# Decays of a Mamba-2 branch from running sums: one DMA per group repeats them on all partitions, instead of matmuls per pair of heads

## The chip, the core and the metric

One NeuronCore of a Trainium2 chip runs the kernel alone. The metric is device time in microseconds, from runs of the whole kernel. Five engines work side by side, each through its own queue in order: PE (TensorE, matmuls), DVE (VectorE) and ACT (ScalarE) for elementwise work, POOL (GpSimd) for elementwise work in SBUF, and SP, which here only issues DMAs.

## What is computed

The reference is one layer of a decoder block on 256 tokens of 2048 features: a sliding-window attention and a Mamba-2 (SSD) branch side by side, then a ConvFFN and a gated embedding. The change lies in the SSD branch alone, which has 64 heads of 64 features in 8 groups of 8 heads, a state of 128, and two chunks of 128 tokens:

```python
a = jnp.moveaxis(dt * A, 2, -1)
a_cum = jnp.cumsum(a, axis=-1)
xdt = x * dt[..., None]
seg = jnp.exp(jnp.where(causal, a_cum[..., :, None] - a_cum[..., None, :], -jnp.inf))
cb = jnp.einsum('bclgn,bcsgn->bcgls', Cm, Bm)
y_diag = jnp.einsum('bcgjls,bcsgjp->bclgjp', cb[:, :, :, None] * seg, xdt)
decay_to_end = jnp.exp(a_cum[..., -1:] - a_cum)
chunk_states = jnp.einsum('bclgn,bcgjl,bclgjp->bcgjpn', Bm, decay_to_end, xdt)
y_off = jnp.einsum('bclgn,bcgjpn,bcgjl->bclgjp', Cm, states_in, jnp.exp(a_cum))
```

`seg` is, for each head, a 128 x 128 matrix of decays between two tokens of a chunk: the exponential of a difference of running sums of `a`. `exp(a_cum)` is the decay from the start of a chunk to each of its tokens.

## The kernel before

All large products are float32 and are made of two matmuls in a rounded format: a weight chunk of 512 KB is loaded (`raw`, five buffers), ACT rounds it (`wh`, three buffers, L77), DVE takes the rest (`wl`, three buffers, L78), and PE multiplies `wh` with both halves of the activations (512 columns, L84) and `wl` with one half (256 columns, L83 or L86). `panel` makes two tiles of 128 features from four such chunks of eight pairs of matmuls; every part of the layer runs through it.

The SSD branch is a loop over 8 groups (L292). Each takes five panels: two for x, one for B and C together, two for the gate z. A panel of x, B or C is evicted by `conv`, with ACT's copy `lo` (L282) first; one of z by `summed` (L112). `step_sizes` (L226) runs once beside the first panels and gives `dt`, `dta` (dt times A, by token) and its rounded halves `dhl`.

For chunk c of a group the kernel then makes E, the decays of all 8 heads (tokens s on the partitions, tokens l along the columns). For each half of four heads and each half of `dhl`, POOL multiplies the mask `tri` with `dhl`, both broadcast, into `rm` (L345, 128 x 512, two buffers), and PE multiplies a strictly lower triangular matrix with it (L347). Their sum in PSUM is the difference of the running sums, and ACT's exponential puts it into E (L348). DVE multiplies E with the masked product of C and B (`cbm`, L349), PE multiplies with `xdt` (L353, eight fp32 matmuls), and DVE adds the skip term (L357).

For the path from chunk 0 into chunk 1, PE makes `po` from the state (L365), and with eight fp32 matmuls (L370) the running sums of chunk 1 for each pair of heads, repeated over 64 partitions each; ACT takes their exponential `ec` (L373), and DVE multiplies and adds (L374, L375). Then follow the gate (L386), the group norm (ACT's square L387, POOL's sums of it L388 and L389, two matmuls L392, POOL's power L396, two matmuls L399, DVE L400) and the split into `YS`.

The order of the instructions on each engine is not the program's: a scheduler with a model of time lays it out (`schedule_with_timeline_sim=True`), so that the small matmuls of the SSD stand among the pairs of the panels. A DMA that ACT issues stands in ACT's queue, and waits there for what it needs.

Of the kernel before, what the change touches and what calls it, by code (L numbers as in the profile page):

```python
# [17 lines left out]
P = 128  # L18
T = 256
# [18 lines left out]
RLEN = 384  # L38
# panels of queries and of gate_a: attention on one pair of heads runs beside the panels that follow it
ATT_ORDER = ([("q", 0), ("q", 1), ("q", 2)] + [x for n in range(5) for x in (("g", n), ("q", n + 3))]  # L40
# [4 lines left out]
def hybrid_block(ctx: ExitStack, tc: tile.TileContext, a: dict, out: bass.AP):  # L45
# [46 lines left out]
    def panel(src, base, nk, xs, before=None, between=None, joined=False):  # L92
        """Two feature tiles of w.T @ x: halves [w*x_hi + w_lo*x_hi | w_hi*x_lo], or joined in one half."""
        ps = [acc(), acc()]
        for j in range(nk // KC):
            if before:
                wh, wl = load_chunk(src[base + j], parts=2, before=lambda i, j=j: before(KC * j + 2 * i))
            else:
                wh, wl = load_chunk(src[base + j])
            for ct in range(2):  # L100
                cs = slice(ct * P, (ct + 1) * P)
                for k in range(KC):
                    (products_joined if joined else products)(
                        ps[ct], wh[:, k, cs], wl[:, k, cs], xs[:, j * KC + k, :],
                        j * KC + k == 0, j * KC + k == nk - 1)
            if between:
                between()
        return ps
# [8 lines left out]
    def split(dst, src):  # L117
        """dst[:, 0:T] + dst[:, T:2T] == src, each part with 12 significant bits."""
        S.activation(dst[:, 0:T], src, AF.Copy)
        V.tensor_tensor(dst[:, T:2 * T], src, dst[:, 0:T].bitcast(F32), ALU.subtract)  # L120
# [7 lines left out]

# [1 line left out]
    g_mix = load_const("g_mix", [P, ND])  # L130
# [22 lines left out]
    def stat_to_rstd(sq_blocks, name):  # L153
        """Rows' mean squares -> [P, 2] rstd by token and [P, T] broadcast over partitions."""
        st = misc()
# [41 lines left out]

# [1 line left out]
    y_pool = tc.alloc_tile_pool(name="yp", bufs=1)  # L199
    YS = y_pool.tile([P, 4 * GROUPS, 2 * T], F32R, name="YS")  # L200
    with tc.tile_pool(name="ssm", bufs=2) as sp:
# [3 lines left out]
        nc.sync.dma_start(sl32, a["slow"])  # L205
        slr = sp.tile([P, P], F32R, name="slr", bufs=1)
        V.tensor_copy(slr, sl32)
        cw = sp.tile([P, 48, 4], F32, name="cw", bufs=1)
# [9 lines left out]

        # dt = softplus(raw + bias), by token
        H = SSM_HEADS  # L220
        dt = sp.tile([P, 2, H], F32, name="dt", bufs=1)
        dta = sp.tile([P, 2, H], F32, name="dta", bufs=1)
        dtd = sp.tile([P, H], F32, name="dtd", bufs=1)
        dhl = sp.tile([P, 2, 2, H], F32R, name="dhl", bufs=1)

        def step_sizes():  # L226
# [25 lines left out]
            for b in range(2):  # L252
                V.scalar_tensor_tensor(xr[:, b, :], psd[:, b * H:(b + 1) * H], r_tok[:, b:b + 1], dtb,
                                       ALU.mult, ALU.add)
            # softplus(x) = max(x, 0) + log1p(e), e = exp(-|x|); log1p(e) = 2 atanh(e / (2 + e))
            e = scr[:, 6 * P:7 * P].rearrange("p (b h) -> p b h", b=2)
# [15 lines left out]
            V.scalar_tensor_tensor(dta, dt, -1.0, bc(ea.unsqueeze(1), [P, 2, H]), ALU.mult, ALU.mult)  # L272
            S.activation(dhl[:, 0], dta, AF.Copy)
            V.tensor_tensor(dhl[:, 1], dta, dhl[:, 0].bitcast(F32), ALU.subtract)
            pst = misc()
# [16 lines left out]
        for g in range(GROUPS):  # L292
            hs = slice(8 * g, 8 * g + 8)
            xc = sp.tile([P, 4, T], F32, name="xc")
            for pn in range(2):
                if g + pn == 0:
                    ps2 = first
                else:
                    ps2 = panel(W, base, ND, XS)
                    base += CH  # L300
                if g + pn == 0:
                    step_sizes()
                for i in range(2):
                    j = 2 * pn + i
                    conv(ps2[i], 4 * g + j, xc[:, j, :])
# [7 lines left out]

            # C.B for s in chunk 0 (both chunks of l), then chunk 1
            pcb = misc()
# [6 lines left out]

            # x by token, times dt
            xdt = sp.tile([P, 2, 512], F32, name="xdt", bufs=1)
# [13 lines left out]
            for c in range(2):  # L338
                E = sp.tile([P, 8, P], F32, name="E", bufs=1)
                for hf in range(2):  # L340
                    h4 = slice(8 * g + 4 * hf, 8 * g + 4 * hf + 4)
                    pe = misc()
                    for w in range(2):
                        rm = sp.tile([P, 4, P], F32R, name="rm", bufs=2)
                        G.tensor_tensor(rm, bc(tri.unsqueeze(1), [P, 4, P]),  # L345
                                        bc(dhl[:, w, c, h4].bitcast(F32).unsqueeze(2), [P, 4, P]), ALU.mult)
                        TE.matmul(pe, lhsT=slr, rhs=rm, start=(w == 0), stop=(w == 1))  # L347
                    S.activation(E[:, 4 * hf:4 * hf + 4, :], pe.rearrange("p (h l) -> p h l", h=4), AF.Exp)  # L348
                V.tensor_tensor(E, E, bc(cbm[:, 2 * c, :].unsqueeze(1), [P, 8, P]), ALU.mult)  # L349
# [9 lines left out]

            # from chunk 0 into chunk 1  # L360
            po = misc()
            pc = misc()
            for j in range(4):
                js = slice(j * P, (j + 1) * P)
                TE.matmul(po[:, js], lhsT=xde[:, js], rhs=cbm[:, 1, :], start=True, stop=True)  # L365
            for j in range(4):
                js = slice(j * P, (j + 1) * P)
                for r in range(2):
                    hd = 8 * g + 2 * j + r
                    TE.matmul(pc[r * HD:(r + 1) * HD, js], lhsT=bc(dta[:, 1, hd:hd + 1], [P, HD]),  # L370
                              rhs=tri, start=True, stop=True)
            ec = sp.tile([P, 512], F32, name="ec", bufs=1)
            S.activation(ec, pc, AF.Exp)  # L373
            V.tensor_tensor(ec, po, ec, ALU.mult)  # L374
            V.tensor_tensor(yg[:, :, P:T], yg[:, :, P:T], ec.rearrange("p (j l) -> p j l", j=4), ALU.add)  # L375

            # gate and group norm
            zg = sp.tile([P, 4, T], F32, name="zg", bufs=2)
# [25 lines left out]

    # gate_s, then the SSD branch's output projection
    t1_pool = tc.alloc_tile_pool(name="t1", bufs=1, side="right")
# [14 lines left out]

# [1 line left out]
    m_pool = tc.alloc_tile_pool(name="mp", bufs=1, side="right")  # L423
# [3 lines left out]
    with tc.tile_pool(name="att", bufs=2) as ap:  # L427
        # bias[q, h, j] for key j of [own block | previous block], each block's keys from last to first;
        # masked outside the window
        tab = ap.tile([N_BUCKETS + 1, N_HEADS], F32, name="tab", bufs=1)  # L430
# [27 lines left out]
        def head_rstd(t, scale, nm):  # L458
            """[P tok, blk, 2 heads]: scale * r / sqrt(r^2 ms + eps) for a tile of two heads."""
            sq = ap.tile([P, T], F32, name="hsq")  # L460
# [14 lines left out]
        def by_token():  # L475
            """A panel's 256 features by token."""
            nonlocal base
# [13 lines left out]

        # keys: normalised, both gains folded in, reversed in each block (block 1 first),
        # copied to both halves of the partitions
        flip = ap.tile([P, P], F32, name="flip", bufs=1)
# [27 lines left out]

        # values by token, reversed in each block
        vt = ap.tile([P, 2, 256], F32, name="vt", bufs=1)
# [8 lines left out]
        def attend(i, qc):  # L533
            """One pair of heads, in steps that are laid between the chunks of later panels."""
            g = i // 4
            bias = pair_bias(i)
            rq = head_rstd(qc, HD ** -0.5, "rq")
            Ls = ap.tile([P, 2, 384], F32, name="Ls", bufs=3)
            # head h: its high part on its own half of the partitions, the low part on the other half
            Q = ap.tile([P, 2, T], F32R, name="Q")  # L540
# [74 lines left out]

    # attention's output projection and the mix
    ms_pool2 = tc.alloc_tile_pool(name="mp2", bufs=1, side="right")
# [13 lines left out]

# [1 line left out]
    x_pool = ctx.enter_context(tc.tile_pool(name="xp", bufs=1))  # L633
# [56 lines left out]

# [1 line left out]
    with tc.tile_pool(name="ple", bufs=2) as pp:  # L692
# [36 lines left out]
def _bucket_onehot():  # L729
    """[33, 384]: column v stands for distance v - 127; the last row marks what lies outside the window."""  # L730
    d = np.arange(MAX_DISTANCE)
# [15 lines left out]
def _panels(w, cols):  # L747
    """w's columns, 256 a panel, as [panels * k-chunks, 128, KC * 256]."""
    k = w.shape[0]
# [15 lines left out]
def _layout(i):  # L765
# [10 lines left out]
    w_in = i["w_in"][0]  # L776
    two = lambda v: np.concatenate([v, v]).reshape(P, 1)  # noqa: E731
    m = {
# [52 lines left out]
```

## Time and profile before

| | before |
|---|---|
| time, median of 3 runs (lowest to highest) | 2137.7 us (2135.12 to 2138.09) |
| span of the profiled execution, first to last instruction | 2133.4 us |
| busy, share of the span: PE, DVE, ACT, POOL | 99%, 71%, 55%, 9% |
| mean granted TensorE clock, share of full speed | 0.996 |
| DMA traffic | 377.04 MB, mean 177 GB/s |

The times are of runs without a profile; of the profiled execution the span is known, and it stands 4.3 us below the median. In the profile's views, the busy time of PE is the sum of its matmul records, which overlap. An fp32 matmul makes two records. The chain of work that ended last follows the program back from its end, at each step to what released it. The idle time of an engine is given with the instruction that ended it. The loop over the SSD groups lies between about 35 and 615 us of the span.

### The profile page before, as it was taken

How to read it: one execution, taken by the hardware profiler on the slowest of the kernel's cores; microseconds unless marked ns; L12 is line 12 of the kernel's file. 1: busy time of each engine (PE TensorE's matmuls, PEld its weight loads, DVE VectorE, ACT ScalarE, POOL GpSimd, SP SyncE). 2: the span in 40 equal slices, each digit the busy share in tenths (PEclk: the TensorE clock that was granted, in tenths of full speed). 3: DMA queues.
4: the chain of work that ended last, by engine and by line, in shares of the span. 5: the costliest groups of instructions: out<-in, count | busy, mean ns of one | idle time of the engine just before them, and what ended most of it. 6: DMA issues, size and time to landing. Idle time of an engine off the chain costs nothing.

```text
span 2133.4 us, 32471 instructions
## 1 busy us (share of the span) xinstructions
PE 2114.2 (99%) x12412; PEld 1833.4 (86%) x12412; DVE 1508.8 (71%) x2528; ACT 1174.8 (55%) x1783; POOL 181.7 (9%) x154
## 2 busy tenths in 40 slices
PE   7999999999999999999999999999999999999999
PEld 5888888888888889888888888888888888888888
DVE  7788888888654455766677677777777776555576
ACT  5665666656554444656565556555555555444454
POOL 3221222211100000000000020000000000000000
PEclk9999999999999999999999999999999999999999
DMA  5444444444455556444435655555555555555564
GB/s 196 168 168 164 164 159 158 166 167 165 154 191 187 186 185 201 153 161 139 160 119 178 227 187 184 191 188 186 186 189 188 186 187 187 188 187 188 178 206 145
DMA packets 112072, 377.04 MB, mean 177 GB/s; under 512 B 13931, under 2 KB 20908, under 8 KB 111788
## 3 DMA queue, kind: packets, MB, share of 16 engines
q1 hardware_dynamic: 104060, 366.00, 49.3%
q10 hardware_dynamic: 7856, 8.97, 1.3%
q8 instruction: 97, 1.59, 0.3%
q14 instruction: 59, 0.48, 0.1%
HBM read 372.78 MB, written 2.15 MB: 176 GB/s over the span
## 4 chain that ended last, share of the span: by engine, by line
PE 99%; DVE 1%; ACT 0%; issue 0%; DMA 0%; POOL 0%; DVEq 0%; ACTq 0%
PE acc L84 59%; PE acc L86 29%; PE acc L83 2%; PE ms L550 1%; PE ms L347 1%; PE ms L353 1%; PE ms L549 1%; PE ms L582 1%; PE acc L90 1%; PE ms L365 0%; PE ms L370 0%; PE ms L589 0%; PE acc L486 0%; PE ms L84 0%; PE acc L487 0%; PE acc L488 0%
## 5 line engine op out<-in xcount | busy, mean ns | idle before, releaser
L78 DVE TENSOR_TENSOR wl<-raw,wh 128x1024 fp32r<-128x1024 f32 (+1 forms) x700 | 863.7, 1234 | 507.3 <-ACT wh L77 495.4
L77 ACT ACTIVATE wh<-raw 128x1024 fp32r<-128x1024 f32 (+1 forms) x700 | 733.2, 1048 | 623.6 <-PE acc L84 445.0
L84 PE MATMUL acc<-XS,wh 128*128 128x512 f32 x2048 | 718.8, 399 | 7.2 <-ACT wh L77 7.1
L84 PE MATMUL acc<-XG,wh 128*128 128x512 f32 x1632 | 559.4, 395 | 0.0
L86 PE MATMUL acc<-XS,wl 128*128 128x256 f32 x1920 | 536.9, 286 | 6.1 <-DVE wl L78 6.1
L84 PEld LDWEIGHTS acc<-XS,wh 128*128 128x128 f32 x2048 | 376.7, 190 | 79.7 <-ACT wh L77 7.7
L86 PE MATMUL acc<-XG,wl 128*128 128x256 f32 x1530 | 413.5, 282 | 0.0
L86 PEld LDWEIGHTS acc<-XS,wl 128*128 128x128 f32 x1920 | 364.2, 190 | 24.4 <-DVE wl L78 9.9
L84 PEld LDWEIGHTS acc<-XG,wh 128*128 128x128 f32 x1632 | 293.6, 188 | 53.8
L86 PEld LDWEIGHTS acc<-XG,wl 128*128 128x128 f32 x1530 | 287.6, 188 | 14.0
L84 PE MATMUL acc<-FS,wh 128*128 128x512 f32 x704 | 245.5, 397 | 0.0
L86 PE MATMUL acc<-FS,wl 128*128 128x256 f32 x688 | 189.9, 282 | 0.0
L84 PE MATMUL acc<-YS,wh 128*128 128x512 f32 x512 | 178.2, 396 | 0.0
L84 PEld LDWEIGHTS acc<-FS,wh 128*128 128x128 f32 x704 | 129.9, 188 | 28.5
L86 PE MATMUL acc<-YS,wl 128*128 128x256 f32 x496 | 137.3, 282 | 0.0
L86 PEld LDWEIGHTS acc<-FS,wl 128*128 128x128 f32 x688 | 129.3, 188 | 2.9
L112 ACT ACTIVATE lo<-acc 128x256 f32<-128x256 f32 x158 | 59.9, 383 | 100.0 <-PE acc L84 99.9
L84 PEld LDWEIGHTS acc<-YS,wh 128*128 128x128 f32 x512 | 94.2, 188 | 20.1
L345 POOL TENSOR_TENSOR rm<-tri,dhl 128x512 fp32r<-128x512 f32 x64 | 87.0, 1374 | 280.7 <-PE ms L347 252.1
L654 POOL TENSOR_TENSOR sqa<-sqa,rsq 128x256 f32<-128x256 f32 x30 | 32.6, 1088 | 883.7 <-ACT rsq L653 882.8
L86 PEld LDWEIGHTS acc<-YS,wl 128*128 128x128 f32 x496 | 93.3, 188 | 2.2
L84 PE MATMUL acc<-AS,wh 128*128 128x512 f32 x256 | 88.6, 397 | 0.2 <-DVE sum L114 0.2
(249 smaller groups left out, 2262.5 us busy)
## 6 DMA issues: line engine op xcount, KB each, us to landing
raw<-in_w_in SPq DMA_DIRECT2D x260, 512.0 KB, 3.2
raw<-in_w_ffn_up SPq DMA_DIRECT2D x176, 512.0 KB, 3.2
raw<-in_w_ffn_down SPq DMA_DIRECT2D x88, 512.0 KB, 3.2
raw<-in_w_ssm_out SPq DMA_DIRECT2D x64, 512.0 KB, 3.2
raw<-in_w_attn_out SPq DMA_DIRECT2D x32, 512.0 KB, 3.3
raw<-in_w_out SPq DMA_DIRECT2D x32, 512.0 KB, 3.2
raw<-in_w_ple_gate SPq DMA_DIRECT2D x32, 512.0 KB, 3.2
bias<-rdr ACTq DMA_DIRECT2D x16, 256.0 KB, 3.4
```

The source lines that it names most:

```text
L77: S.activation(wh[:, ks, :], raw[:, ks, :], AF.Copy)
L78: V.tensor_tensor(wl[:, ks, :], raw[:, ks, :], wh[:, ks, :].bitcast(F32), ALU.subtract)
L83: TE.matmul(ps[:, 0:T], lhsT=wl, rhs=x[:, 0:T], start=False, stop=False, skip_group_check=True)
L84: TE.matmul(ps, lhsT=wh, rhs=x, start=first, stop=last)
L86: TE.matmul(ps[:, 0:T], lhsT=wl, rhs=x[:, 0:T], start=False, stop=False, skip_group_check=True)
L90: TE.matmul(ps[:, 0:T], lhsT=w, rhs=x[:, h * T:(h + 1) * T], start=first and n == 0, stop=last and n == 2)
L112: S.activation(lo, ps[:, T:2 * T], AF.Copy)
L345: G.tensor_tensor(rm, bc(tri.unsqueeze(1), [P, 4, P]), bc(dhl[:, w, c, h4].bitcast(F32).unsqueeze(2), [P, 4, P]), ALU.mult)
L347: TE.matmul(pe, lhsT=slr, rhs=rm, start=(w == 0), stop=(w == 1))
L353: TE.matmul(py[r * HD:(r + 1) * HD, j * P:(j + 1) * P], lhsT=xdt[:, c, h * HD:(h + 1) * HD], rhs=E[:, h, :], start=True, stop=True)
L549: TE.matmul(ss[h][:, cs], lhsT=Q[:, h, qs], rhs=kh[g][:, ks], start=True, stop=False)
L654: G.tensor_tensor(sqa, sqa, sq, ALU.add)
```

## The change

The running sums themselves are made once, in `step_sizes`, by four fp32 matmuls: `acs`, by token on the partitions (for the subtracted term), and `ach`, by head on 64 partitions, which ACT copies from PSUM and stores to a DRAM tile `acd` of 64 KB. For each group, ACT issues one DMA that reads the sums of the group's 8 heads for both chunks (8 KB) into every one of the 128 partitions: `acb`, 128 x 2048, 1 MB, one buffer. E is then `acb - acs` and its product with the mask, two POOL operations on 128 x 1024 (L359, L360 of the new code), an exponential in place on ACT (L361, 128 x 1024), and DVE's product as before (now L362). `ec` is the exponential of rows of `acb`, in two ACT instructions of 64 partitions (L381). The matmuls of L347 and L370, `rm`, `dhl` and `slr` are gone. In the new code the products with `xdt` are L366, the state's L377, the group norm's matmuls L400 and L407, the group's transposes L346 (before: L353, L365, L392, L399, L329).

```diff
-        slr = sp.tile([P, P], F32R, name="slr", bufs=1)
-        V.tensor_copy(slr, sl32)
...
-        dhl = sp.tile([P, 2, 2, H], F32R, name="dhl", bufs=1)
+        acs = sp.tile([P, 2, H], F32, name="acs", bufs=1)
+        acd = dram.tile([H, 2 * P], F32, name="acd")
+
+        def sums_of_group(g):
+            t = sp.tile([P, 8, 2, P], F32, name="acb", bufs=1)
+            nc.scalar.dma_start(t, bass.AP(acd.tensor, acd.offset + 8 * g * 2 * P, [[0, P], [2 * P, 8], [P, 2], [1, P]]))
+            return t
...
-            S.activation(dhl[:, 0], dta, AF.Copy)
-            V.tensor_tensor(dhl[:, 1], dta, dhl[:, 0].bitcast(F32), ALU.subtract)
+            psa = misc()
+            for c in range(2):
+                TE.matmul(psa[:, c * H:(c + 1) * H], lhsT=tri, rhs=dta[:, c, :], start=True, stop=True)
+            S.activation(acs, psa[:, 0:2 * H].rearrange("p (c h) -> p c h", c=2), AF.Copy)
+            pah = misc()
+            for c in range(2):
+                TE.matmul(pah[0:H, c * P:(c + 1) * P], lhsT=dta[:, c, :], rhs=tri, start=True, stop=True)
+            ach = sp.tile([H, 2 * P], F32, name="ach", bufs=1)
+            S.activation(ach, pah[0:H, 0:2 * P], AF.Copy)
+            nc.scalar.dma_start(acd, ach)
...
         for g in range(GROUPS):
             hs = slice(8 * g, 8 * g + 8)
+            if g:
+                acb = sums_of_group(g)
...
                 if g + pn == 0:
                     step_sizes()
+                    acb = sums_of_group(0)
...
             for c in range(2):
                 E = sp.tile([P, 8, P], F32, name="E", bufs=1)
-                for hf in range(2):
-                    h4 = slice(8 * g + 4 * hf, 8 * g + 4 * hf + 4)
-                    pe = misc()
-                    for w in range(2):
-                        rm = sp.tile([P, 4, P], F32R, name="rm", bufs=2)
-                        G.tensor_tensor(rm, bc(tri.unsqueeze(1), [P, 4, P]),
-                                        bc(dhl[:, w, c, h4].bitcast(F32).unsqueeze(2), [P, 4, P]), ALU.mult)
-                        TE.matmul(pe, lhsT=slr, rhs=rm, start=(w == 0), stop=(w == 1))
-                    S.activation(E[:, 4 * hf:4 * hf + 4, :], pe.rearrange("p (h l) -> p h l", h=4), AF.Exp)
+                sa = bc(acs[:, c, hs].unsqueeze(2), [P, 8, P])
+                G.tensor_tensor(E, acb[:, :, c, :], sa, ALU.subtract)
+                G.tensor_tensor(E, E, bc(tri.unsqueeze(1), [P, 8, P]), ALU.mult)
+                S.activation(E, E, AF.Exp)
                 V.tensor_tensor(E, E, bc(cbm[:, 2 * c, :].unsqueeze(1), [P, 8, P]), ALU.mult)
...
             po = misc()
-            pc = misc()
...
-            for j in range(4):
-                js = slice(j * P, (j + 1) * P)
-                for r in range(2):
-                    hd = 8 * g + 2 * j + r
-                    TE.matmul(pc[r * HD:(r + 1) * HD, js], lhsT=bc(dta[:, 1, hd:hd + 1], [P, HD]),
-                              rhs=tri, start=True, stop=True)
             ec = sp.tile([P, 512], F32, name="ec", bufs=1)
-            S.activation(ec, pc, AF.Exp)
+            for r in range(2):
+                rows = slice(r * HD, (r + 1) * HD)
+                S.activation(ec[rows, :].rearrange("p (j l) -> p j l", j=4), acb[rows, r::2, 1, :], AF.Exp)
```

The rest of the diff removes comments. The scheduler lays the program out anew; behind the SSD stage the order of PE is the same as before, and two places within it matter here. The first is POOL in the loop. Before, from the start of the SSD stage through the first group (two of the ten `rm` are the next group's):

```order
L164 TENSOR_TENSOR rt_mix<-tiny_a,mhalf 128x2
L345 TENSOR_TENSOR rm<-tri,dhl 128x512 x10
L388 TENSOR_TENSOR zg<-zg 128x512
L389 TENSOR_TENSOR zg<-zg 128x256
L396 TENSOR_TENSOR rg<-msg,mhalf 128x2
```

And now, from chunk 1 of one group to chunk 1 of the next (the numbers tell the buffers' tiles apart; acb_2168 holds the sums of one group, acb_2798 those of the next):

```order
L359 TENSOR_TENSOR E_2545<-acb_2168,acs_297 128x1024
L360 TENSOR_TENSOR E_2545<-E_2545,tri_280 128x1024
L359 TENSOR_TENSOR E_3157<-acb_2798,acs_297 128x1024
L360 TENSOR_TENSOR E_3157<-E_3157,tri_280 128x1024
L396 TENSOR_TENSOR zg_2573<-zg_2573 128x512
L397 TENSOR_TENSOR zg_2573<-zg_2573 128x256
L404 TENSOR_TENSOR rg_2784<-msg_2782,mhalf_89 128x2
L359 TENSOR_TENSOR E_3175<-acb_2798,acs_297 128x1024
```

The third and fourth rows belong to chunk 0 of the next group: they now stand ahead of the group norm's sums. E has one buffer, so each subtraction waits until PE has multiplied with the E before it.

The second place is ACT, around the end of a group's chunk 1 (`wh` is a weight chunk for PE, `lo` an eviction, `zg<-yg` the square for the group norm). Before:

```order
L373 ACTIVATE ec<-ms 128x512 [waits PE_49]
L77 ACTIVATE wh<-raw 128x1024 [waits DMAHW1_49,PE_49,Activation_49]
L77 ACTIVATE wh<-raw 128x1024 [waits DMAHW2_49,PE_49,Activation_49]
L387 ACTIVATE zg<-yg 128x1024 [waits DVE_49]
L77 ACTIVATE wh<-raw 128x1024 [waits DMAHW3_49,PE_49,Activation_49]
```

And now, in the same place of a group:

```order
L381 ACT_TABLE_LOAD [waits DMAHW5_49]
L381 ACTIVATE ec<-acb 64x512 [waits DVE_49]
L381 ACTIVATE ec<-acb 64x512
L296 ACTIVATE lo<-acc 128x256 [waits PE_49]
L395 ACTIVATE zg<-yg 128x1024 [waits DVE_49,Activation_49]
L361 ACTIVATE E<-E 128x1024 [waits Pool_49]
L296 ACTIVATE lo<-acc 128x256 [waits PE_49]
L77 ACTIVATE wh<-raw 128x1024 [waits DMAHW6_49,Activation_49]
```

`ec` and E here are already those of the next group. E waits for POOL, and an eviction and the next `wh` stand behind it. The DMA itself stands further up in ACT's queue:

```order
L77 ACTIVATE wh<-raw 128x1024 [waits DMAHW7_49,PE_49,Activation_49]
L77 ACTIVATE wh<-raw 128x1024 [waits DMAHW0_49,PE_49,Activation_49]
L229 DMA acb<-acd 128x2048 [waits Pool_49]
L112 ACTIVATE lo<-acc 128x256 [waits PE_49] x2
L77 ACTIVATE wh<-raw 128x1024 [waits DMAHW1_49,DVE_49]
L361 ACT_TABLE_LOAD
L361 ACTIVATE E<-E 128x1024 [waits Pool_49]
```

It waits until POOL has read the sums of the group at hand for chunk 1, with two evictions and a `wh` behind it; nothing of the kind stood there before.

## Rows read from the trace of the kernel before

**Rows 1.** The page: busy time of each engine; the last chain by engine.
```profile
PE 2114.2 (99%) x12412; PEld 1833.4 (86%) x12412; DVE 1508.8 (71%) x2528; ACT 1174.8 (55%) x1783; POOL 181.7 (9%) x154
...
PE 99%; DVE 1%; ACT 0%; issue 0%; DMA 0%; POOL 0%; DVEq 0%; ACTq 0%
```

**Rows 2.** Windows, one group: us; busy PE, PEld, DVE, ACT, POOL; clock, DMA, GB/s.
```profile
284.08:349.16 65.08, 65.08 (x406) 56.54 (x408) 53.46 (x89) 40.47 (x55) 13.84 (x11) 1.00 0.47 163
```

**Rows 3.** PE's waits, whole run: who for whom, us in total, times, longest.
```profile
PE acc L84 <- ACT wh L77: 7.1, 2, 5.7
PE acc L86 <- DVE wl L78: 6.1, 4, 2.3
PE ms L167 <- POOL rt_mix L164: 1.0, 1, 1.0
```

**Rows 4.** The chain in one group: start us, us, what.
```profile
285.10 0.66 PE ms L347 x2
...
290.12 0.24 PE ms L347
...
291.29 0.23 PE ms L347
...
299.23 1.02 PE ms L370 x16
300.25 0.32 PE acc L86
...
302.89 0.12 PE acc L86
303.01 0.24 PE acc L84
```

**Rows 5.** POOL by line, duration ns min/median/max; costliest groups, busy us, mean ns.
```profile
L345 POOL TENSOR_TENSOR rm<-tri,dhl x64: 1037/1042/2112, 60.9 to 546.9; 128x512 fp32r<-128x512 f32 x64
L388 POOL TENSOR_TENSOR zg<-zg x8: 1372/1377/1559, 108.4 to 566.8; 128x512 f32<-128x512 f32 x8
L345 POOL TENSOR_TENSOR rm<-tri,dhl 128x512 fp32r<-128x512 f32 x64 | 87.0, 1374 | 280.7 <-PE ms L347 252.1
```

**Rows 6.** Timeline of POOL, 337 to 350 us: start us, us, instruction.
```profile
342.49 3.87 POOL L345 TENSOR_TENSOR rm<-tri,dhl 128x512 fp32r<-128x512 f32 x2 [2.78 <-PE ms L347]
```

**Rows 7.** Timeline of DVE, the same stretch.
```profile
344.23 1.23 DVE L349 TENSOR_TENSOR E<-E,cbm 128x1024 f32<-128x1024 f32 x1 [0.83 <-ACT E L348]
345.44 2.00 DVE L78 TENSOR_TENSOR wl<-raw,wh 128x1024 fp32r<-128x1024 f32 x1
```

**Rows 8.** Timeline of ACT, first group.
```profile
58.54 1.06 ACT L306 ACTIVATE xc<-xc 128x1024 f32<-128x1024 f32 x1
...
61.86 0.38 ACT L282 ACTIVATE lo<-acc 128x256 f32<-128x256 f32 x1 [0.80 <-PE acc L84]
...
64.29 1.10 ACT L288 ACTIVATE BC<-u,cb__288,cw 128x256 f32<-128x256 f32 x2 [1.10 <-DVE u L286]
65.40 1.28 ACT L277 ACT_TABLE_LOAD   x1
66.70 0.22 ACT L277 ACTIVATE dtd<-ms 128x64 f32<-128x64 f32 x1
```

**Rows 9.** ACT by line: duration ns min/median/max; the second is an issue.
```profile
L348 ACT ACTIVATE E<-ms x32: 597/599/601, 75.8 to 551.9; 128x512 f32<-128x512 f32 x32
L444 ACTq DMA_DIRECT2D bias<-rdr x16: 366/366/488, 828.4 to 1044.5; - x16
```

**Rows 10.** DMA issues from ACT's queue: KB each, median us from issue to landing.
```profile
bias<-rdr ACTq DMA_DIRECT2D x16, 256.0 KB, 3.4
...
X<-in_xT ACTq DMA_DIRECT2D x1, 2048.0 KB, 9.3
...
rdr<-rsb ACTq DMA_DIRECT2D x1, 48.0 KB, 3.0
```

**Rows 11.** The chain over the run: start us, us, what (the first group's transposes).
```profile
73.44 0.87 PE ms L329 x8
```

## The prediction

> **What bounds the kernel now.** I read the page's busy table and chain first. TensorE (PE) is busy 99% of the span, and the chain of work that ended last is 99% PE [rows 1]. Then I asked whether this holds in the stage that the change touches, the loop over eight groups, with the windows view: one group takes 65.08 us, and PE is busy in all of it, DVE in 53.46, ACT in 40.47, POOL in 13.84, at a granted clock of 1.00 [rows 2]. All waits of PE for ACT's `wh` in the whole run come to 7.1 us and those for DVE's `wl` to 6.1 [rows 3], hence what PE is spared in this stage shortens the run until another engine comes late. The reader should take two things from this: PE's issue time is the currency, and any saving can be eaten only by new waits of PE.
>
> The busy table is the wrong place for the price of a matmul: a record of 512 columns there lasts about 0.4 us because matmuls overlap. The chain gives what each one takes from its successor [rows 4]: 0.23 to 0.24 us for 512 columns, 0.12 us for 256, so 0.352 us for the usual pair (one `wh`, one `wl` matmul) and 8 x 0.352 = 2.8 us for a chunk of weights.
>
> **What PE loses and gains.** Removed per group: eight matmuls of L347 and eight fp32 matmuls of L370. A chunk's four of L347 take 0.66 + 0.24 + 0.23 us in the chain [rows 4]. Of the 0.66 for the first two, 2 x 0.23 is theirs; the other 0.2 is what any wide matmul pays behind the 64-row matmuls of L353, and it stays. So 0.46 + 0.24 + 0.23 = 0.93, twice per group, 1.87. L370's 16 records (two for each fp32 matmul) take 1.02 us, and the 256-column matmul behind them 0.32 in place of 0.12 [rows 4]; after the change the 128-row matmuls of L377 stand there, so this 0.2 goes too: 1.22. Sum per group 3.09, for eight groups 24.7 us.
>
> The Trainium skill prices this lower: TensorE: Matmul & The Clock Gate, section Back-to-back issue gap, has a sustained spacing of about 131 ns at 512 columns and 81 ns at 128. By it I would estimate 64 x 0.131 + 128 x 0.081 = 18.8 us. The spacing in the chain decides, and it disagrees with both figures.
>
> Added, once, in `step_sizes`: four fp32 matmuls of at most 128 columns. L370's 1.02 us for eight says 0.13 each [rows 4], so 0.5 us. PE's balance: 24.2 us less, about 62.0 us per group.
>
> **What moves on the other engines, and what covers it.**
> POOL: 64 operations on 512 columns become 32 on 1024. One of the old ones takes 1.04 us undisturbed, 2.11 at worst [rows 5]. The new subtraction and masking read a whole tile where `rm` read two broadcast ones; the nearest such operation, L388, takes 1.377 for 512 columns [rows 5], 1.32 times as long. Two `rm` took 3.87 us together at one place [rows 6], where twice 1.04 would be undisturbed; beside them a DVE instruction on 1024 columns took 2.00 in place of 1.23 [rows 7], so the two engines hold each other up. Hence for one new operation, p: at least 2 x 1.04 = 2.1 us, at most 2 x 2.11 x 1.32 = 5.6. I take 3.2, between twice the 512-column mean with its disturbances (87.0 / 64 x 2 = 2.7 [rows 5]) and that times 1.32 (3.6).
>
> Two stretches then decide whether PE waits. First, from chunk 0's product (L366) to chunk 1's PE has 31 or 32 pairs, 31.5 x 0.352 = 11.1 us. In that time POOL must subtract and mask (2p), ACT take the exponential (1.06, as for other tiles of 1024 columns [rows 8]), DVE finish half a `wl` (0.6) and multiply (1.23 [rows 7]): 2p + 2.9, a wait of 2p - 8.2 if positive. At 3.2 it is covered by 1.8 us. Second, the scheduler now makes chunk 0's E of the next group right behind chunk 1's product. ACT's exponential waits for it, and weight chunks stand behind it in ACT's queue. From that product PE has about 10.2 us until it needs the first such `wh`, and 0.4 more until its `wl`; the chain is 2p, exponential 1.06, `wh` 1.06 [rows 8], `wl` 1.23 [rows 7], hops and an eviction of 0.38 [rows 8], 2p + 3.8: a wait of 2p - 6.8. At 3.2 it is covered, by only 0.4 us. This is the narrowest cover in the change.
>
> ACT: the exponentials of a group were four of 0.6 us and one of 0.6 for `ec` [rows 9]; now two of 1.06 and two of 0.6 (as many columns on half the rows), 3.3 for 3.0, plus the issue of one DMA, 0.37 [rows 9]. ACT stands idle 24.6 us of each group [rows 2]; the cost without that cover would be 0.7 x 8 = 5.6 us. Queued behind the DMA issue, which now waits for POOL to have read the old sums, are evictions and a `wh`; PE then still has two chunks, 5.6 us, against about p + 1 us of waiting. Covered.
>
> DVE loses one subtraction and one copy in the whole run, worth nothing while DVE idles. DMA: eight loads of 1 MB. 256 KB from ACT's queue landed after 3.4 us and 2 MB after 9.3 [rows 10]; I take 5.2 for 1 MB, and the program issues each some 9 us before its readers come, so late groups hide it even at 9.3.
>
> The first group cannot. In the trace its ACT work for `BC` ends at 65.39 us [rows 8]; two copies from PSUM (0.38 each at most), a table load 1.28, `dtd` 0.22 [rows 8] and an issue 0.37 bring the store of the sums to 68.0; a store of this kind landed after 3.0 [rows 10], the load after another 0.4 + 5.2, so 76.6. Then 2p, 1.06, 0.6 and 1.23: 85.9 at p = 3.2, 83.7 at the least p. PE came to the transposes of this group at 73.44 [rows 11]; in the new order they stand some five pairs earlier and behind the four added matmuls, thus about 72.0, and the product comes 0.9 us of transposes and 29 pairs, 10.2 us, later: 83.1. The wait is 0.6 to 2.8 us, with a load of 9.3 up to 6.9. I take 1.5, since POOL meets little DVE work there.
>
> **Sum.** Against the profiled execution: 2133.4 - 24.7 + 0.5 + 1.5 = 2110.7 us of span. The median of the runs shown, 2137.7, stands 4.3 us above that span, and I carry these over: **2115.0 us**. The low end, 2111, is no wait in the first group and the 0.2 behind L353 gone as well (16 x 0.2 = 3.2, of which I allow 2.5).
>
> **Rivals.** (A) *Part of the gain is given back at the narrow cover.* With p = 4.0 the two waits are 1.2 and 0 us per group, 10 us in all: 2125; with 4.2 they are 1.6 and 0.2, 14 us: 2129. For it: DVE is busy 82% of a group [rows 2] and will be 86% of the shorter one, and a POOL operation twice as long meets more of DVE's. Against it: in the whole run before, POOL ended one wait of PE, of 1.0 us and outside this stage [rows 3].
>
> (B) *POOL becomes the pace-maker, slower.* Place: E of the next group, with `wh` queued behind it in ACT's queue. Eight groups have 24.2 - 1.5 = 22.7 us to give, 2.8 each; (2p - 6.8) + (2p - 8.2) = 2.8 gives p = 4.45 as the point of no gain. At 5.5, near the upper bound, the waits are 7.0 us a group, 56 us: 2171. For it: the worst `rm` on record, 2.11 us, doubled and with full operands gives 5.6. Against it: that takes a collision in each operation, where the mean says 2.7 to 3.6. By GPSIMD Engine Reference of the Trainium skill, section Key points, POOL contends with every DVE instruction that has two SBUF inputs; the `wl` that took 2.00 us beside `rm` agrees.
>
> (C) *The loads of the sums land late*, because 128 partitions read the same 8 KB. Nothing in the trace is that shape at that size. Past 9 us each further one costs 7 groups one us: a landing after 12 us gives 2115 + 21 + 5 for the first group, 2141, no change.
>
> **How the numbers follow.** Forecast, all covered but the first group (2111 to 2120): 0.60. A (2120 to 2133): 0.25. C and the mild end of B, within 0.2%: 0.07. B in earnest: 0.08. A difference under 0.2%, 4.3 us here, is about what a measurement of this kernel cannot tell from none. So faster 0.85, same 0.07, slower 0.08. The range of 2111 to 2131 holds the forecast and nearly all of A, and leaves out C, B and a little below.
>
> **What would show it.** Right: the stage's groups 62 us apart, PE without idle time in them, POOL operations of about 3 us, PE's one new wait at the first L366. Wrong: PE idle before L366, before L400 or before an L84 whose `wh` came from behind L361; groups still 65 us apart; loads of `acb` over 9 us.

## The result and the profile after

| | before | after |
|---|---|---|
| time, median of 4 runs each (lowest to highest) | 2137.89 us (2135.12 to 2138.33) | 2113.34 us (2112.45 to 2114.96) |
| span of the profiled execution | 2133.4 us | 2111.6 us |

The ratio is 0.9887, 95% interval 0.9875 to 0.9899: the kernel is 24.6 us (1.1%) faster.

The page answers to [rows 1]: the busy times of the engines, the last chain by engine, and the new DMA (KB each, median us from issue to landing).

```profile
PE 2094.0 (99%) x12228; PEld 1815.8 (86%) x12228; DVE 1511.2 (72%) x2526; ACT 1176.4 (56%) x1775; POOL 182.6 (9%) x122
...
PE 96%; issue 1%; DVE 1%; DMA 1%; ACT 0%; POOL 0%; SPq 0%; ACTq 0%; POOLq 0%
...
acb<-acd ACTq DMA_DIRECT2D x8, 1024.0 KB, 6.3
```

PE binds as before. The chain's share of PE is lower because it runs over other engines in more of the first 34 us, and for some 15 us at each of two short waits of PE in the loop (below). DVE and POOL, with different instructions, are busy as long as before. The windows view, from `po`'s matmuls (L377) behind one chunk 1 product to those of three groups later, answers to [rows 2] (us; busy PE, PEld, DVE, ACT, POOL; clock, DMA, GB/s):

```profile
156.88:343.14 186.26, 186.09 (x1141) 161.96 (x1141) 161.67 (x264) 122.12 (x160) 41.20 (x21) 1.00 0.54 187
```

A group takes 186.26 / 3 = 62.09 us in place of 65.08. That is 2.99 us less, with PE busy in all but 0.17 us of the three groups; DVE is busy 53.9 of 62.1. PE's waits in the whole run answer to [rows 3] and are no longer than before:

```profile
PE acc L84 <- ACT wh L77: 7.0, 2, 5.6
PE acc L86 <- DVE wl L78: 4.6, 6, 2.0
PE ms L167 <- POOL rt_mix L164: 1.0, 1, 1.0
```

In the chain, `po`'s matmuls now follow a chunk's product, and the 256-column matmul behind them takes 0.12 us where it took 0.32 behind L370 [rows 4]; once, the sums' matmuls are added:

```profile
64.44 0.39 PE ms L281 x4
64.83 0.58 PE ms L285 x4
...
155.85 1.02 PE ms L366 x16
156.88 1.09 PE ms L377 x8
157.96 0.12 PE acc L86
```

The two POOL operations of E by line (ns, min/median/max) answer to [rows 5]:

```profile
L359 POOL TENSOR_TENSOR E<-acb,acs x16: 1898/1899/2871, 73.7 to 517.4; 128x1024 f32<-128x1024 f32 x16
...
L360 POOL TENSOR_TENSOR E<-E,tri x16: 2408/2770/3498, 76.7 to 519.4; 128x1024 f32<-128x1024 f32 x16
```

Together they take 4.67 us by the medians, 2.33 us each, where the prediction took p = 3.2; by the mean it is 2.50 (79.9 us for the 32).

**The narrow place.** Between 60 and 590 us PE waits twice, 0.17 us each:

```profile
PE acc L86 <- DVE wl L78: 0.3, 2, 0.2
```

Both waits stand where the prediction put its narrowest cover, behind chunk 1's product with E of the next group on POOL, in two of the eight groups. For the first of them, at 295 us, this is POOL's timeline, then DVE's (start us, us, instruction, idle before it):

```profile
283.72 2.73 POOL L359 TENSOR_TENSOR E<-acb,acs 128x1024 f32<-128x1024 f32 x1 [8.16 <-PE ms L366]
286.53 2.79 POOL L360 TENSOR_TENSOR E<-E,tri 128x1024 f32<-128x1024 f32 x1
```

```profile
285.65 0.68 DVE L382 TENSOR_TENSOR ec<-ms,ec 128x512 f32<-128x512 f32 x1
286.36 0.69 DVE L383 TENSOR_TENSOR yg<-yg,ec 128x512 f32<-128x512 f32 x1
287.09 3.32 DVE L394 TENSOR_TENSOR yg<-yg,zg 128x1024 f32<-128x1024 f32 x1
290.33 1.21 DVE L78 TENSOR_TENSOR wl<-raw,wh 128x1024 fp32r<-128x1024 f32 x1
...
294.02 1.21 DVE L78 TENSOR_TENSOR wl<-raw,wh 128x1024 fp32r<-128x1024 f32 x1
```

The product with the gate took 3.32 us. It started 0.56 us after POOL's masking and ended 1.09 after POOL's end, so it seems to have stood still while POOL worked. By line (ns, min/median/max), the same product before and after:

```profile
L386 DVE TENSOR_TENSOR yg<-yg,zg x8: 1215/1222/1224, 104.6 to 564.1; 128x1024 f32<-128x1024 f32 x8
```

```profile
L394 DVE TENSOR_TENSOR yg<-yg,zg x8: 1211/3244/3320, 100.4 to 532.0; 128x1024 f32<-128x1024 f32 x8
```

Before, it was never held up. Behind it DVE has a `wl`, two evictions and then the `wl` of 294.02, for which PE waits. The windows view of this stretch shows a DVE without a gap:

```profile
282.30:295.30 13.00, 12.84 (x88) 10.81 (x86) 12.83 (x16) 9.74 (x14) 7.63 (x4) 1.00 0.38 124
```

ACT's queue, by which the prediction counted, was held up by the same product:

```profile
290.50 1.06 ACT L395 ACTIVATE zg<-yg 128x1024 f32<-128x1024 f32 x1 [0.77 <-DVE yg L394]
291.47 1.04 ACT L361 ACTIVATE E<-E 128x1024 f32<-128x1024 f32 x1
...
292.68 1.05 ACT L77 ACTIVATE wh<-raw 128x1024 fp32r<-128x1024 f32 x1
```

The square for the group norm stands ahead of E's exponential in that queue and needs the gate's product. So the exponential began 2.2 us after POOL's end, and the `wh` behind it ended at 293.73, 0.3 us before DVE took it up. The margin here was DVE's, and it was used up at 2p = 5.5 us (2.73 + 2.79). The prediction put its end at 6.8, by way of ACT alone and without the square.

### The profile page after: what moved, and what is told of

The parts are those of the page before. It is cut to its first block, busy times and chain, and to the rows that moved or that the text cites. A ratio compares the mean times of both kernels' runs of the same rounds, so it can differ in the third digit from the quotient of the medians.

```text
span 2111.6 us, 32047 instructions
## 1 busy us (share of the span) xinstructions
PE 2094.0 (99%) x12228; PEld 1815.8 (86%) x12228; DVE 1511.2 (72%) x2526; ACT 1176.4 (56%) x1775; POOL 182.6 (9%) x122
## 4 chain that ended last, share of the span: by engine, by line
PE 96%; issue 1%; DVE 1%; DMA 1%; ACT 0%; POOL 0%; SPq 0%; ACTq 0%; POOLq 0%
PE acc L84 59%; PE acc L86 28%; PE acc L83 2%; PE ms L558 1%; PE ms L557 1%; PE ms L366 1%; PE ms L590 1%; PE acc L90 1%; DVE wl L78 0%; PE ms L597 0%; PE ms L84 0%; PE ms L472 0%; PE ms L346 0%; PE ms L377 0%; PE ms L599 0%
## 5 line engine op out<-in xcount | busy, mean ns | idle before, releaser
L84 PE MATMUL acc<-MS,wh 128*128 128x512 f32 x256 | 87.7, 396 | 0.0
```

The source lines that it names most:

```text
L84: TE.matmul(ps, lhsT=wh, rhs=x, start=first, stop=last)
```

## The experiments

Every kernel is the changed one with the edit shown. Medians are compared with the runs of before on the same chip: the first four rows ran on one chip, the next four on a second, the last four on a third. The runs of one kernel lie 2 to 7 us apart, those of pool_side 14. after_again is the level for differences below, also across chips, where before moved by 1 us.

| kernel | us | before | ratio (95% interval) |
|---|---|---|---|
| after_again | 2114.67 | 2137.67 | 0.9893 (0.9880 to 0.9907) |
| dead512 | 2130.55 | 2137.67 | 0.9970 (0.9959 to 0.9981) |
| dead64 | 2123.95 | 2137.67 | 0.9940 (0.9928 to 0.9952) |
| part_E | 2122.32 | 2137.67 | 0.9935 (0.9922 to 0.9949) |
| part_ec | 2129.38 | 2138.65 | 0.9955 (0.9943 to 0.9968) |
| pool1 | 2145.78 | 2138.65 | 1.0035 (1.0023 to 1.0047) |
| pool2 | 2169.00 | 2138.65 | 1.0140 (1.0125 to 1.0156) |
| min0 | 2113.38 | 2138.65 | 0.9880 (0.9866 to 0.9893) |
| pool58 | 2128.02 | 2137.80 | 0.9953 (0.9936 to 0.9969) |
| pool_side | 2140.99 | 2137.80 | 1.0016 (1.0004 to 1.0028) |
| act_lat | 2130.62 | 2137.80 | 0.9966 (0.9954 to 0.9978) |
| dve_E | 2114.32 | 2137.80 | 0.9889 (0.9874 to 0.9904) |

### What a matmul is worth

after_again has no edit. 

> The changed kernel once more, as the level that the kernels beside it are set against: 2113.3 us, 24.5 below the kernel before, by every theory.

It came to 2114.67 us, 23.0 below before. The next three ran beside it.

dead512:

```diff
+                pd = misc()
+                for w in range(4):
+                    TE.matmul(pd, lhsT=XS[:, w, 0:P], rhs=XS[:, w, :], start=True, stop=True)
                 sa = bc(acs[:, c, hs].unsqueeze(2), [P, 8, P])
```

> The changed kernel, with four more matmuls of 512 columns per chunk of a group (64 in the run, as many as L347 had) on operands that are ready; their result is not read. Theory, PE's issue time is the currency: the price is that of L347 in the chain, 0.23 to 0.24 us each, 64 x 0.234 = 15.0, so 2128.3 us, and PE is busy throughout. Rival, the gain came from the other engines or from the new layout: no change, 2113. By the Trainium skill, TensorE: Matmul & The Clock Gate, section Back-to-back issue gap, 131 ns each: 64 x 0.131 = 8.4, so an estimate of 2121.7.

Measured: 15.9 us over after_again, 0.25 us for each of the 64. The chain shows four of them behind full-width matmuls and four behind the product with `xdt`:

```profile
331.32 0.93 PE ms L360 x4
...
337.17 1.02 PE ms L369 x16
338.19 1.12 PE ms L360 x4
```

0.93 / 4 is the 0.23 of [rows 4], and 16 x 0.93 is 14.9 us; the last 1.0 us is within the spread of the runs. The other 0.19 is the share that the prediction left with whatever wide matmul comes behind the 64-row ones. The estimate of 8.4 us by the Trainium skill lies outside the measurement, and the rival with no change falls.

dead64:

```diff
+            pc = misc()
+            for j in range(4):
+                js = slice(j * P, (j + 1) * P)
+                for r in range(2):
+                    hd = 8 * g + 2 * j + r
+                    TE.matmul(pc[r * HD:(r + 1) * HD, js], lhsT=bc(dta[:, 1, hd:hd + 1], [P, HD]),
+                              rhs=tri, start=True, stop=True)
             ec = sp.tile([P, 512], F32, name="ec", bufs=1)
```

> The changed kernel, with the eight fp32 matmuls of L370 back in each group (64 in the run, two records each), their result not read; ec stays the exponential of the sums. Theory: 1.02 us per group by the chain of the kernel before, and up to 0.2 more where a 256-column matmul follows them: 8.2 to 9.8 us, so 2121.5 to 2123.1. Rival, small matmuls hide in gaps that PE has anyway: 2113. By the same page of the Trainium skill, 81 ns a record: 128 x 0.081 = 10.4, so an estimate of 2123.7.

Measured: 9.3 us more, inside the range from the chain; these small matmuls did not hide. The 10.4 by the Trainium skill lies too near to be told apart.

part_E has the same eight matmuls, and `ec` is made from them:

```diff
-            for r in range(2):
-                rows = slice(r * HD, (r + 1) * HD)
-                S.activation(ec[rows, :].rearrange("p (j l) -> p j l", j=4), acb[rows, r::2, 1, :], AF.Exp)
+            S.activation(ec, pc, AF.Exp)
```

> The change for E alone: E from the repeated sums, ec again from the eight matmuls of L370. Theory: the changed kernel plus 8.2 to 9.8 us for L370: 2121.5 to 2123.1; the difference from the kernel before is then L347's 15.0 less 0.97 for the four added matmuls, 14 to 16 us. Rival, ACT's two exponentials of 64 rows for ec, or POOL, hold something up: below that by more than a us.

part_ec makes E by `rm` and L347 as before; the DMA brings chunk 1's sums alone:

```diff
-            t = sp.tile([P, 8, 2, P], F32, name="acb", bufs=1)
+            t = sp.tile([P, 8, P], F32, name="acb", bufs=1)
...
-                S.activation(ec[rows, :].rearrange("p (j l) -> p j l", j=4), acb[rows, r::2, 1, :], AF.Exp)
+                S.activation(ec[rows, :].rearrange("p (j l) -> p j l", j=4), acb[rows, r::2, :], AF.Exp)
```

> The change for ec alone: E again from rm and L347, ec from the repeated sums of chunk 1 (512 KB for each group). Theory: the kernel before less 8.2 to 9.8 us for L370, plus 0.5 for the two added matmuls: 2128.5 to 2130.1, and with the change for E alone the two parts add up to the whole. Rival, the two parts share a gain (PE is freed once, by either): nearer to 2137 or to 2115.

Measured: the change for E alone gains 15.4 us (2137.67 - 2122.32), that for `ec` alone 9.3 (2138.65 - 2129.38). Their sum is 24.6; the whole is 24.6 in the first measurement and 23.0 in after_again. Within such differences the parts add up. The two parts do not share a gain, and each is worth about what its matmuls cost when put back (dead512, dead64).

### How far POOL is covered

pool1 masks twice, pool2 three times, and pool58 masks five of the eight heads a second time. The edit of pool1:

```diff
                 G.tensor_tensor(E, E, bc(tri.unsqueeze(1), [P, 8, P]), ALU.mult)
+                G.tensor_tensor(E, E, bc(tri.unsqueeze(1), [P, 8, P]), ALU.mult)
```

> The changed kernel, with the masking on POOL done twice, which leaves the result as it is. By the durations in the changed kernel's trace, 2p goes from 4.7 to about 7.4 us. Theory, the two formulas of the prediction (waits 2p - 6.8 and 2p - 8.2): 0.6 us per group, so 2118 us. Rival, the scheduler knows of the longer work and moves the products away from it: 2113 to 2115.

> The changed kernel, with the masking on POOL done three times. 2p becomes about 10.2 us. By the two formulas with PE's order kept: 3.4 and 2.0 us per group, 43 in all, so 2157 us, slower than before: this is the prediction's slower rival made real. Rival, the scheduler lays the order out anew (chunk 0 and chunk 1 of a group stand about 90 pairs of matmuls apart on PE instead of 60 to 66) and hides it: 2113 to 2125.

> The changed kernel, with five of the eight heads masked a second time on POOL: 2p goes from 4.7 to about 6.4 us, the value that the prediction took (p = 3.2). The prediction's formulas: no wait, 2113.3 us. The repeated masking of all eight heads cost 32 us for 2.7 us more of POOL work per E; on a straight line that would be 2113.3 + 1.7 x 12 = 2133. Theory now: POOL's work stops DVE for as long as it lasts (two runs: POOL 38.6 and 78.0 us more, DVE 43.4 and 76.7 us more), so 3.4 us more of DVE per group and a time between, 2118 to 2133.

All three took longer than the formulas say (2113, 2118 and 2157 us), and pool58 ended between the formulas and the straight line. By the medians of their own POOL rows, 2p was 6.2 us in pool58 (1.90 + 2.44 + 1.91), 7.2 in pool1 and 10.2 in pool2. So at 3.1, a little under the prediction's own p of 3.2, the time is 2128.0 us, not 2113; at 7.2 / 2 it is 2145.8, slower than before. These kernels reach their 2p by a third POOL instruction and have orders of their own; as far as they stand for a larger p, rival B is real, and it comes early: a line from 2128.0 to 2145.8 meets the time before, 2138, at 2p of some 6.8, p = 3.4, where the prediction put that point at 4.45. In pool2 the scheduler set the products of a group further apart (18 to 20 us for 12), and the time still rose past the forecast.

pool1 shows how. This is POOL's timeline, then DVE's, of two stretches some 15 us apart:

```profile
282.94 2.41 POOL L360 TENSOR_TENSOR E<-E,tri 128x1024 f32<-128x1024 f32 x1
285.43 3.26 POOL L361 TENSOR_TENSOR E<-E,tri 128x1024 f32<-128x1024 f32 x1
...
299.55 2.48 POOL L360 TENSOR_TENSOR E<-E,tri 128x1024 f32<-128x1024 f32 x1
302.10 2.74 POOL L361 TENSOR_TENSOR E<-E,tri 128x1024 f32<-128x1024 f32 x1
```

```profile
283.30 3.13 DVE L78 TENSOR_TENSOR wl<-raw,wh 128x1024 fp32r<-128x1024 f32 x1 [1.26 <-ACT wh L77]
...
286.80 2.17 DVE L393 TENSOR_TENSOR zg<-sum,rb_mix 128x256 f32<-128x256 f32 x1
...
300.38 2.19 DVE L384 TENSOR_TENSOR yg<-yg,ec 128x512 f32<-128x512 f32 x1
302.50 2.63 DVE L304 SCALAR_TENSOR_TENSOR xc<-u,cw,xc 128x256 f32<-128x256 f32 x1
...
306.91 1.21 DVE L78 TENSOR_TENSOR wl<-raw,wh 128x1024 fp32r<-128x1024 f32 x1
```

`wl` starts, but ends only 1.08 us after POOL's masking, which ended at 285.35: it looks as if it waited inside itself. Meanwhile the second masking, started at 285.43, takes 3.26 us where the first took 2.41. Then `zg`, 0.43 us elsewhere, takes 2.17 and ends 0.28 after POOL's end. The times are those of two engines that take turns, an instruction at a time. In the second stretch L384 and L304, which take 0.69 and 0.48 us in the changed kernel (there L383 and L304), lose 1.5 and 2.2 us in the same way, and end 0.5 and 0.3 us after the POOL instruction beside them. The `wl` of 306.91 stands behind them in DVE's queue, and PE waits for it. PE's timeline and the windows view around this wait:

```profile
308.18 0.52 PE L86 MATMUL acc<-XS,wl 128*128 128x256 f32 x1 [2.90 <-DVE wl L78]
```

```profile
307.00:308.20 1.20, 0.02 (x1) 0.03 (x1) 1.20 (x2) 1.20 (x2) 0.44 (x1) 1.00 0.00 0
308.20:313.50 5.30, 5.30 (x22) 4.60 (x23) 5.26 (x7) 3.04 (x4) 1.86 (x2) 0.68 0.48 154
```

PE stands still for 2.90 us for want of `wl`. Behind that the granted clock is 0.68 for 5.3 us, part of it at the lower of the two levels, 1.2 GHz; by an estimate that is another 5.3 x 0.32 = 1.7 us. PE's waits in the loop add up to 23.2 us in this run, and PE's busy time is 7.2 us longer for the same 12228 matmuls (2101.2 against 2094.0). Together that is 30.4 us, the difference of the two spans (2142.0 - 2111.6).

pool_side was to put as much POOL work outside the chain, act_lat to make the chain as much longer without POOL:

```diff
                 S.activation(E, E, AF.Exp)
+                for hf in range(2):
+                    side = sp.tile([P, 4, P], F32, name="side", bufs=1)
+                    G.tensor_tensor(side, acb[:, 4 * hf:4 * hf + 4, c, :], bc(tri.unsqueeze(1), [P, 4, P]), ALU.mult)
```

```diff
                 S.activation(E, E, AF.Exp)
+                S.activation(E, E, AF.Copy)
+                S.activation(E, E, AF.Copy)
+                S.activation(E[:, 0:4, :], E[:, 0:4, :], AF.Copy)
```

> The changed kernel, with as much more POOL work as one more masking per E (four products of 128x512 per group, of the sums and the mask, into a tile that nothing reads), but outside the chain that makes E: POOL does it as soon as the sums have landed. Theory, POOL stops DVE: DVE's busy time up by about 40 us as with the repeated masking, and the time well above 2113, up to 2145. Rival, the length of the chain through E is what costs: 2113 to 2116. Between them lies a mixed case: the hold-up costs only where DVE's work is urgent.

> The changed kernel, with three copies of E in place on ACT behind the exponential (two of 1024 columns, one of 512): the chain through E is 2.65 us longer, as with one more masking on POOL, and ACT has 5.3 us more of work per group, of some 20 idle, but POOL and DVE do nothing more. Theory, POOL's hold-up of DVE is what costs: 2113 to 2120, DVE's busy time within 5 us of 1511. Rival, the length of the chain is what costs: 2140 to 2150, as with the repeated masking.

pool_side came to 2141.0 us, with DVE's busy time at 1545.6, 34 more. But its work did not stay outside the chain. This is POOL around the end of a group:

```profile
294.38 7.12 POOL L364 TENSOR_TENSOR side<-acb,tri 128x512 f32<-128x512 f32 x4 [5.38 <-DMA acb<-acd]
301.48 1.89 POOL L359 TENSOR_TENSOR E<-acb,acs 128x1024 f32<-128x1024 f32 x1
```

The four products that nothing reads stand in POOL's queue ahead of the next group's E. PE's product that frees E began at 295.97; in the changed kernel the subtraction starts 1.2 us after that (283.72 behind 282.54), here it came 4.3 us later still, and in six groups 1.1 to 4.5. The added work also took 53.2 us of POOL, where the second masking cost 38.6. So this run has both causes in it, and it does not show what POOL work costs that nobody waits for. act_lat came to 2130.6, with DVE at 1525.3: neither theory's range holds it. A longer chain costs too, but the copies stood spread out in ACT's queue (from 239.72 to 252.17 us in one group), so this chain grew by more than one masking. The two prices, 26 and 16 us, do not add up to pool1's 31. The scheduler laid each of these kernels out anew, so a clean split between the two causes stays open.

dve_E:

```diff
-                G.tensor_tensor(E, acb[:, :, c, :], sa, ALU.subtract)
-                G.tensor_tensor(E, E, bc(tri.unsqueeze(1), [P, 8, P]), ALU.mult)
+                V.tensor_tensor(E, acb[:, :, c, :], sa, ALU.subtract)
+                V.tensor_tensor(E, E, bc(tri.unsqueeze(1), [P, 8, P]), ALU.mult)
```

> The changed kernel, with the subtraction and the masking of E on DVE instead of POOL. Theory, POOL stops DVE for as long as it works: DVE loses 79.9 us of hold-up and gains 32 instructions of 1.23 us, 39.4, so its busy time is about 1471 us in place of 1511, POOL's 103; the time as before or a little less, 2111 to 2114, since PE binds. Rival, the hold-up is partial and DVE, busy 87% of a group, has no room for 4.9 us more per group: DVE at 1550, waits of PE for wl, 2125 to 2145.

The time was as expected, 2114.32 us, with no wait of PE in the loop; the busy time was not. The page, and DVE's two new lines:

```profile
PE 2092.1 (99%) x12228; PEld 1814.8 (86%) x12228; DVE 1519.4 (72%) x2558; ACT 1176.3 (56%) x1775; POOL 101.8 (5%) x90
```

```profile
L359 DVE TENSOR_TENSOR E<-acb,acs x16: 1215/1216/1225, 73.3 to 521.8; 128x1024 f32<-128x1024 f32 x16
...
L360 DVE TENSOR_TENSOR E<-E,tri x16: 1210/1212/1217, 77.7 to 523.6; 128x1024 f32<-128x1024 f32 x16
```

DVE took over 32 x 1.213 = 38.8 us and is busy 8.2 us longer, so on balance 30.6 us of stalls went away (35.4 against after_again, whose DVE was busy 1516.0 us, so such a difference is good to some 5 us). The 79.9 us of E on POOL had thus cost DVE some 0.4 us for each, not one for one. The second masking of pool1 cost 43.4 for 38.6. The reading that fits both, but that no run tests alone, is that a us of POOL stops DVE only while DVE has something to do that POOL excludes, and that this was so all the time only in the crowded stretch.

min0:

```diff
-                G.tensor_tensor(E, E, bc(tri.unsqueeze(1), [P, 8, P]), ALU.mult)
+                G.tensor_scalar(E, E, 0.0, None, ALU.min)
```

> The changed kernel, with a minimum with 0 in place of the masking on POOL (above the diagonal the difference of the sums is never below zero, so that the exponential is 1 there in either way, and cbm takes it out). It reads one operand instead of two. Theory: POOL is covered, so no change of the time, 2113.3 within 1 us, the POOL instruction shorter than 2.77 us, and PE's two waits of 0.17 us for wl in the SSD stage gone. Rival, POOL's work costs PE something by way of DVE that the waits do not show: over 2 us faster.

The time is the same, 2113.38 us, and the two waits are gone, but not for the reason given: the instruction is no shorter.

```profile
L360 POOL TENSOR_SCALAR E<-E x16: 2770/2936/3859, 78.7 to 522.7; 128x1024 f32<-128x1024 f32 x16
```

DVE's product with the gate has a median of 1.94 us in this run and 3.24 in the changed kernel, and DVE is busy 9.7 us less. Why one operand fewer holds DVE up less is left open.

No run beat the changed kernel; dve_E and min0 equal it. Two buffers for E or `acb` were not tried.

## Why the prediction came true, step by step

- **PE's issue time is the currency**: held. A group is shorter by what PE no longer issues, part by part (part_E, part_ec), and longer by what is put back (dead512, dead64).
- **3.09 us per group**: measured 2.99, of which 0.06 is PE's wait; 23.9 us for eight. The price from the chain, 0.23, held.
- **Added matmuls, 0.5 us**: the step that was mis-sized. L281 and L285 take 0.39 + 0.58 = 0.97 us. L370's 0.13 each was the wrong model; these took 0.24 each.
- **p = 3.2**: too high. The maskings were near L388's price, 2 x 1.377, but the subtraction of a broadcast operand took 1.90, less than two `rm` (2 x 1.04).
- **The narrowest cover, 2p - 6.8**: the right place, the wrong path and too long a cover. It counted E's exponential and the `wh` behind it on ACT, and left out the square ahead of them, which waits for DVE. What ended last was DVE, with the product with the gate held up by POOL and the evictions and `wl` behind it, and nothing was left at 2p = 5.5. The prediction knew the hold-up from [rows 6, 7] and put it into p alone, not into DVE's queue.
- These two errors cancelled, and that was luck. With a cover that ends at 5.5, 2p = 6.4 would by this count cost PE 0.9 us more at each such place, even in the changed kernel's own order (an estimate; no run has this order with a larger p). pool58, which has an order of its own, took 2128.0 us at 6.2. That is the far end of rival A's times, which the prediction reached only at p = 4.2. The 0.60 for "all covered" was too bold for the margin that was there.
- **First group, a wait of 1.5 us**: none. The store left at 65.85 us, while ACT loaded a table, and not at 68.0; the first load landed 4.3 us after its issue, the shortest of the eight (median 6.3), where the prediction took 5.2; and 2p was 5.3. So the first E was ready before PE came, which itself came 1.5 us later than forecast. This is DVE's product, and PE's in the chain:

```profile
80.74 1.21 DVE L362 TENSOR_TENSOR E<-E,cbm 128x1024 f32<-128x1024 f32 x1
```

```profile
84.67 1.02 PE ms L366 x16
```

- **Sum**: 2110.7 us of span forecast, 2111.6 measured, with terms that were off in both directions: -24.7 + 0.5 + 1.5 = -22.7 forecast, -23.9 + 1.0 + 0 = -22.9 by the rows, and -21.8 from span to span. The median, 2113.3, stood 1.7 us above the span, not 4.3. In the runs on record a time stands 1.7 to 2.6 us above its own span; the 4.3 held besides that what the profiled run of before was faster than its median. Hence 2113.3 in place of 2115.0.
- **Rival C**: no. The longest of the eight loads landed 7.9 us after its issue, inside the 9 that the order left.

## What to carry to other kernels

Price a matmul by what it takes from its successor in the chain, not by its record: here that forecast 24.2 us of PE time, and the change measured 23.0 to 24.6. When the instructions of an engine grow longer and it holds up another, as POOL did DVE in [rows 6, 7], put their time into both queues: a cover counted along one chain was spent by an instruction on a third engine. A forecast that comes true is tested by setting the assumed value, not the lucky one: near the assumed p (pool58) the time is 13 to 15 us longer.

## What the runs showed of the chip

By the times above, POOL and DVE took turns, instruction by instruction, where DVE's instruction read two operands from SBUF: `wl` 3.13 us in place of 1.22, the gate's product 3.32 in place of 1.21, POOL's masking 3.26 in place of 2.41. DVE's `ec` from PSUM ran beside POOL in 0.68 us, as it does elsewhere. The Trainium skill, GPSIMD Engine Reference, section Key points, names contention of POOL with DVE instructions that have two SBUF inputs, without a time; these rows agree. A wait of PE cost more than itself: behind one of 2.90 us the granted clock was 0.68 over 5.3 us, and in pool_side, behind one of 3.13 us, 0.67 over 5.1. On POOL, a subtraction and a product over the same 128 x 1024 took 1.90 and 2.41 us at the least, so the operation and its operands matter there, not the size alone.
